# A WKV kernel on one core: k loads issued from GpSimd four pairs ahead, and the state chain in 12 VectorE operations a stage over four slots

## The chip, the core and the metric

The kernel runs on one core of a Trainium2 chip. The metric is the device time of one execution in microseconds (us); executions of one kernel differ by one to two per cent. An execution over 1.5% above the fastest of its kernel is counted as slow. All times compared here are of the state called fast, in which the core's mean granted TensorE clock is 0.96 to 0.99 of full speed. Where executions were slow, the text says so and gives the fast ones.

The engines are TensorE (PE; its weight loads are PEld), VectorE (DVE), ScalarE (ACT), GpSimd (POOL) and SyncE (SP). L258 is line 258 of the kernel that was profiled. The changed kernel has other line numbers.

## The reference, cut to what matters

```python
# k, v, out: (16, 2048, 256), float32; w, u: (256,)
for b in range(batch):
    aa, bb, pp = 0, 0, -1e38                  # per channel
    for t in range(seq_len):
        ww = u + k[b, t];  qq = max(pp, ww)
        e1, e2 = exp(pp - qq), exp(ww - qq)
        out[b, t] = (e1 * aa + e2 * v[b, t]) / (e1 * bb + e2 + 1e-08)
        ww = pp - w + k[b, t];  qq = max(ww, k[b, t])
        e1, e2 = exp(ww - qq), exp(k[b, t] - qq)
        aa, bb, pp = e1 * aa + e2 * v[b, t], e1 * bb + e2, qq
```

This is a weighted sum over all earlier steps, kept in range by a running maximum. The weight falls by `w` with each step.

## The kernel before

The kernel takes the 2048 steps in chunks of 126 (two halves of 63). One chunk of all 16 sequences is a **stage**. A stage has four **pairs** of four sequences each, and one pass of the main loop, a **slot**, brings one new pair in and takes an older one (ten slots back) out. The prediction calls the four slots of a stage A, B, C and D. In each slot:

- VectorE rounds k to float32r (`round_k`, "the k cast", L258), casts v to bf16 (L285), multiplies the exponentials by v (L293), and multiplies numerators by reciprocals, two halves per pair (L483).
- TensorE makes the logarithms of the weights (`X`, L266), sums per half chunk (`tot`, L323), numerators (`num`, L475) and denominators (`den`, L457).
- ScalarE makes `ez = exp(X)` (L277) and the reciprocal as exp(-ln) (L465, L466).

Between stages a state per sequence, channel and half chunk is carried on by small VectorE operations of 32 to 128 columns. The sums are turned by TensorE, so that channels lie along partitions (`turn_sums`, L339), and copied (`tsum`, L346). Logarithms give offsets `S`, exponentials of the offsets give weights, and the chain makes the state `AB`. The state is weighted again, turned back and put by four small DMAs into rows of `ez`, where the next outputs use it.

```python
def state_offsets(c):                         # five operations in slot A
    ...
    K(DVE.tensor_copy(S[:, 0, :], st.pop((c - 1, "S"))[:, 2, :]))
    for h in range(2):
        K(DVE.scalar_tensor_tensor(S[:, h + 1, :], S[:, h, :], 0.0, lf[:, h, :], ALU.max, ALU.add))
    K(DVE.tensor_scalar(ex[:, 0:2, :], S[:, 1:3, :], -1.0, 0.0, ALU.mult, ALU.max))
    K(DVE.scalar_tensor_tensor(ex[:, 2:4, :], S[:, 1:3, :], 0.0, lf, ALU.max, ALU.subtract))
...
def state_chain(c):                           # five operations in slot A
    ...
    K(DVE.tensor_mul(tb, t, g[:, 2:4, :]...))
    for h in range(2):
        dst = cur[:, :, 1, :] if h == 0 else nxt[:, :, 0, :]
        K(DVE.tensor_mul(da, cur[:, :, h, :], g[:, h:h + 1, :]...))
        K(DVE.tensor_add(dst, da, tb[:, :, h, :]))
...
def inject_min(c):                            # two operations at the end of slot A
    K(DVE.tensor_scalar(m, st.pop((c, "y")), -0.5, 0.5 * (CAP - LNRS), ALU.mult, ALU.add))
    K(DVE.scalar_tensor_tensor(m2, st[c, "S"][:, 0:2, :], 0.0, m, ALU.max, ALU.min))
...
def carries(c):                               # two multiplies in slot B
    for h in range(2):
        K(DVE.tensor_mul(ab[:, h]..., cur[:, :, h, :]..., f[:, h, :]...))
...
# when it runs: s = last slot of stage c
work += [(s + 1, "last", split_sums), (s + 2, "first" if c else "exp", state_logs),
         (s + 2, "sums", state_offsets), (s + 2, "sums", state_weights), (s + 2, "pool", state_chain),
         (s + 2, "act", inject_logs), (s + 3, "first", inject_min), (s + 3, "exp", inject_weights),
         (s + 3, "pool", carries), (s + 3, "last", turn_carries), (s + 3, "last", inject)]
```

The order within a slot is fixed by the main loop. Every operation is pinned behind the one before it on its engine.

```python
for n in range(NP + LAG + 1):
    load(n + AHEAD)                           # k and v, both issued by SP
    small_work(n, "first");  exps(n);  small_work(n, "exp")
    sums(n - 1);  round_k(n + 1);  small_work(n, "sums")
    num(qp, 0);  den(q);  recip(q);  mult(qp, 0);  num(qp, 1)
    small_work(n, "pool")
    times_v(n);  mult(qp, 1);  store(qp)      # stores: GpSimd; so are the row injections
    logs(n + 1);  cast_v(n + 1)
    small_work(n, "dve");  small_work(n, "act");  small_work(n, "last")
```

## Time and profile before

The median of three executions was 352.86 us (352.79 to 353.68). The profiled one took 353.72 us at a mean clock of 0.965.

| before, 352.0 us span | |
|---|---|
| busy: TensorE, VectorE, ScalarE, GpSimd | 82%, 84%, 79%, 28% |
| period of one stage (four k casts) | 18.67 us |
| spacing of the k casts in A, B, C, D | 6.27, 4.33, 3.53, 4.54 us |
| from the k cast at 85.73 us to the last, 48 casts (twelve stages) later | 223.36 us |
| DMA rate in one stage | 332 GB/s |

The whole-span shares say little, since three engines and the DMA engines all lie between 79 and 89%. The useful unit is the stage, and in it the question is which engine waits for which. The prediction reads those views. These lines are the timeline of VectorE in slot A and of TensorE in slot C (start, duration, engine, line, operation, output<-inputs with shapes and count; idle time just before and its releaser stand in brackets if there was any):

```profile
118.92 0.28 DVE L387 TENSOR_TENSOR tb<-tsum,g 128x128 f32<-128x128 f32 x1
...
119.89 0.22 DVE L392 TENSOR_TENSOR AB<-da,tb 128x64 f32<-128x64 f32 x1
120.03 1.22 DVE L293 TENSOR_TENSOR ez<-ez,vb 126x2048 bf16<-126x2048 bf16 x1
...
125.91 0.40 PE L323 MATMUL tot<-ez,OHE 128*48 128x512 bf16 x1
...
128.39 0.38 PE L475 MATMUL num<-ez,LfN 128*128 128x512 bf16 x1
```

The chain lasts from 118.92 to 120.03, where the v multiply (L293) begins, or 1.11 us.

### The profile page before, as it was taken

The numbers are of one execution on the slowest core, as the hardware profiler recorded it, in microseconds if no ns is written. First come the engines' busy times: TensorE is split into PE (matmuls) and PEld (weight loads), VectorE is DVE, ScalarE is ACT, GpSimd is POOL, SyncE is SP. The second block draws the span as 40 slices with busy tenths as digits, with TensorE's granted clock in tenths as the row PEclk, the third lists the DMA queues.
The fourth block names the chain that finished last, engine by engine and source line by source line (L and its number), as shares of the span: only waits on it lengthen the run. The fifth ranks groups of instructions, "written<-read, shape, count | busy, mean of one in ns | idle before, by whom it ended". The sixth has DMA issues, their size and how long they took to land.

```text
span 352.0 us, 4191 instructions
## 1 busy us (share of the span) xinstructions
PE 290.1 (82%) x1200; PEld 139.0 (39%) x1200; DVE 297.2 (84%) x636; ACT 278.8 (79%) x286; POOL 100.0 (28%) x164
## 2 busy tenths in 40 slices
PE   0578977788989898998989897979798989887870
PEld 0325433343434444444434353534354444433320
DVE  2666787889999999999999999999999999986551
ACT  2465557778988989898989888898888898987880
POOL 5000006131414140414233140514141405142630
PEclk9995689999999999999999999999999999999995
DMA  7899677699999989999999999999999999533774
GB/s 221 202 354 304 190 236 223 214 303 305 321 361 337 371 298 372 299 369 309 351 345 330 349 323 345 327 338 339 354 326 361 304 330 307 208 121 119 225 236 130
DMA packets 81366, 102.59 MB, mean 291 GB/s; under 512 B 5504, under 2 KB 73152, under 8 KB 81344
## 3 DMA queue, kind: packets, MB, share of 16 engines
q1 hardware_dynamic: 68160, 67.58, 60.3%
q0 software_dynamic: 12496, 34.11, 27.8%
q10 hardware_dynamic: 688, 0.66, 0.8%
q8 instruction: 9, 0.15, 0.2%
q14 instruction: 13, 0.11, 0.1%
HBM read 68.22 MB, written 33.55 MB: 289 GB/s over the span
## 4 chain that ended last, share of the span: by engine, by line
PE 40%; DVE 28%; issue 4%; ACT 3%; DMA 2%; POOLq 0%; DVEq 0%
PE num L475 11%; PE X L266 10%; DVE rd L483 8%; PE den L457 7%; PE tot L323 7%; DVE km L258 5%; DVE ez L293 5%; PE den L339 4%; DVE vb L285 2%; DVE AB L392 2%; DMA ez<-row 2%; ACT rd L466 2%; ACT rd L465 1%; DVE da L391 1%; DVE S L366 1%
## 5 line engine op out<-in xcount | busy, mean ns | idle before, releaser
L277 ACT ACTIVATE ez<-X 128x2048 bf16<-128x2048 f32 x66 | 122.2, 1852 | 22.8 <-PE X L266 22.8
L499 POOL DMA_DIRECT2D out_dram<-rd x64 | 58.6, 916 | 195.5 <-DVE rd L483 67.9
L483 DVE TENSOR_TENSOR rd<-num,rd 126x512 f32<-126x512 f32 (+1 forms) x131 | 88.6, 682 | 12.6 <-ACT rd L466 8.4
L293 DVE TENSOR_TENSOR ez<-ez,vb 126x2048 bf16<-126x2048 bf16 (+1 forms) x66 | 79.8, 1209 | 7.9 <-ACT ez L277 6.5
L465 ACT ACTIVATE rd<-den 126x1024 f32<-126x1024 f32 (+1 forms) x66 | 66.8, 1012 | 19.9 <-PE den L457 19.9
L466 ACT ACTIVATE rd<-rd 126x1024 f32<-126x1024 f32 (+1 forms) x66 | 69.5, 1052 | 2.1
L475 PE MATMUL num<-ez,LfN 128*128 128x512 bf16 x128 | 48.9, 382 | 21.4 <-DVE rd L483 20.8
L266 PE MATMUL X<-km,NLE 128*128 128x512 f32 x128 | 54.0, 505 | 15.1 <-DVE km L258 12.7
L323 PE MATMUL tot<-ez,OHV 126*48 126x512 bf16 x128 | 51.0, 399 | 8.5 <-DVE ez L293 8.5
L258 DVE CAST km<-kr 126x1024 fp32r<-126x1024 f32 x64 | 50.7, 792 | 4.6 <-ACT km L192 4.6
L323 PE MATMUL tot<-ez,OHE 128*48 128x512 bf16 x128 | 51.9, 405 | 0.0
L475 PE MATMUL num<-ez,IdN 126*128 126x512 bf16 (+1 forms) x131 | 49.8, 380 | 0.0
L285 DVE CAST vb<-vr 126x1024 bf16<-126x1024 f32 (+1 forms) x66 | 44.7, 677 | 3.3 <-DMA vr<-in_v_dram 3.3
L433 POOL DMA_DIRECT2D ez<-row x64 | 33.0, 520 | 46.7 <-DVE km L258 46.7
L266 PE MATMUL X<-km,NLZ 128*128 128x512 f32 x128 | 41.9, 410 | 0.0
L457 PE MATMUL den<-ez,Id 126*128 126x512 bf16 (+1 forms) x131 | 39.6, 382 | 0.0
L457 PE MATMUL den<-ez,Lf 128*128 128x512 bf16 x128 | 38.1, 378 | 1.5 <-DMA ez<-row 1.5
L266 PEld LDWEIGHTS X<-km,NLE 128*128 128x128 f32 x128 | 24.8, 201 | 28.7 <-DVE km L258 9.6
L475 PEld LDWEIGHTS <-IdN 126*128 126x128 bf16 (+1 forms) x131 | 12.7, 97 | 40.0 <-issue 38.6
L266 PEld LDWEIGHTS X<-km,NLZ 128*128 128x128 f32 x128 | 25.4, 199 | 6.1
L323 PEld LDWEIGHTS <-OHE 128*48 128x48 bf16 x128 | 13.4, 104 | 33.8 <-issue 27.0
L475 PEld LDWEIGHTS <-LfN 128*128 128x128 bf16 x128 | 12.3, 96 | 31.4 <-issue 22.7
(95 smaller groups left out, 199.5 us busy)
## 6 DMA issues: line engine op xcount, KB each, us to landing
out_dram<-rd POOLq DMA_DIRECT2D x64, 504.0 KB, 7.2
kr<-in_k_dram SPq DMA_DIRECT2D x60, 512.0 KB
vr<-in_v_dram SPq DMA_DIRECT2D x59, 512.0 KB
kr<-in_k_dram SPq DMA_DIRECT2D x4, 504.0 KB
vr<-in_v_dram SPq DMA_DIRECT2D x4, 504.0 KB
ez<-row POOLq DMA_DIRECT2D x64, 8.0 KB, 6.9
vr<-in_v_dram ACTq DMA_DIRECT2D x1, 512.0 KB
kr<-in_k_dram SPq DMA_DIRECT2D x3, 128.0 KB
```

The costliest lines, as they stand in the source:

```text
L258: K(DVE.tensor_copy(KM[n][0:r, 0:i, :], kr_of.pop(n)[0:r, 0:i, :]))
L266: K(PE.matmul(X[:, q, i, :], m[0:kr, :], km[0:kr, i, :], start=True, stop=True))
L277: K(SC.activation(ez_of(n)[:, 0:4:2], X_of.pop(n)[:, :, 0:i, :], ACT.Exp))
L285: K(DVE.tensor_copy(vb[0:r, 0:i, :], vr_of.pop(n)[0:r, 0:i, :]))
L293: K(DVE.tensor_mul(ez[0:r, 1:4:2], ez[0:r, 0:4:2], vb[0:r, 0:i, :].unsqueeze(1).broadcast_to([r, 2, i, D])))
L323: K(PE.matmul(TOT[c], m[0:r, :], ez_of(n)[0:r, q, i, :], start=n == first_of[c] and i == 0 and q == 0, stop=n == last_of[c] and i == tiles ...
L457: K(PE.matmul(d[:, i, :], m[0:r, :], ez_of(n)[0:r, q, i, :], start=q == 0, stop=q == 2, skip_group_check=True))
L465: K(SC.activation(rd[0:r, 0:i, :], DEN.pop(n)[0:r, 0:i, :], ACT.Ln, scale=RS))
L466: K(SC.activation(rd[0:r, 0:i, :], rd[0:r, 0:i, :], ACT.Exp, scale=-1.0))
L475: K(PE.matmul(d, m[0:r, :], ez_of(n)[0:r, q, i, :], start=q == 1, stop=q == 3, skip_group_check=True))
L483: K(DVE.tensor_mul(RD[n][0:r, i, :], NUM.pop((n, i))[0:r, :], RD[n][0:r, i, :]))
L499: K(POOL.dma_start(out=out[4 * p:4 * p + 4, t0:t0 + TC, :].rearrange("n t d -> t n d"), in_=o[0:TC, :, :]))
```

## The change

The change has two parts. First, k loads go out on GpSimd's queue, four pairs ahead with four buffers, where they went on SP's queue three ahead with four. The row injections go to SP in exchange. Second, the state chain is rewritten. Offsets stay in one tile for all stages (no copy), and the exponentials become exponentials of one clamped offset. Minima and maxima are folded into the multiplies that use them, and the `m` pair goes. The second step of the chain is moved to slot C. The intent is fewer VectorE operations per stage, set where they hurt less. The core of the diff, with the head of the sequence and unchanged lines left out:

```diff
-    AHEAD = 3
+    AHEAD = 4
-    kpool = ...(name="kpool", bufs=AHEAD + 1)       # vpool likewise
+    kpool = ...(name="kpool", bufs=AHEAD)
-            for t, x, eng in ((kr, k, SP), (vr, v, SP if n else SC)):
+            for t, x, eng in ((kr, k, SP if n <= AHEAD else POOL), (vr, v, SP if n else SC)):
 ...
+    S = consts.tile([128, 2 * NST + 1, 32], F32, tag="S", name="S")
     def state_offsets(c):
-        (copy S, two S, two ex: see above)
+        for h in range(2):
+            i = 2 * c + h
+            K(DVE.scalar_tensor_tensor(S[:, i + 1], S[:, i], 0.0, lf[:, h], ALU.max, ALU.add))
+        K(DVE.tensor_scalar(near, S[:, 2 * c:2 * c + 3], NEAR, -NEAR, ALU.min, ALU.max))
     def state_weights(c):
-        K(SC.activation(g[:, sl, :], st.pop((c, "ex"))[:, sl, :], ACT.Exp, scale=-2.0))
+            K(SC.activation(w, near[:, 0:2], ACT.Exp, scale=-2.0))
+            K(SC.activation(g, near, ACT.Exp, scale=2.0))
-    def state_chain(c):
-        (tb, then da and AB twice: see above)
+    def state_step(c, h):
+        if h == 0:
+            K(DVE.scalar_tensor_tensor(tb, by_two(st.pop((c, "w"))), 1.0, t, ALU.min, ALU.mult))
+        ...
+        K(DVE.tensor_add(da, cur[:, :, h], st[c, "tb"][:, :, h]))
+        K(DVE.scalar_tensor_tensor(cur[:, :, 1] if h == 0 else AB[c + 1][:, :, 0],
+                                   by_two(st[c, "g"][:, h + 1]), 1.0, da, ALU.min, ALU.mult))
-    def inject_min(c):
-        (m, m2: see above)
     def inject_weights(c):
-        K(SC.activation(f, st.pop((c, "m")), ACT.Exp, scale=2.0))
+        K(SC.activation(f, st.pop((c, "y")), ACT.Exp, scale=-1.0, bias=cc[:, 5:6]))
     def carries(c):
-        for h in range(2):
-            K(DVE.tensor_mul(ab[:, h]..., cur[:, :, h, :]..., f[:, h, :]...))
+        K(DVE.scalar_tensor_tensor(f2, st[c, "g"][:, 0:2], 1.0, f, ALU.max, ALU.min))
+        K(DVE.tensor_mul(ab, AB[c]..., f2...))
     def inject(c):
-                K(POOL.dma_start(out=EZ[group_of(c, j)]...
+                K(SP.dma_start(out=EZ[group_of(c, j)]...
 ...
-                     (s + 2, "sums", state_offsets), (s + 2, "sums", state_weights), (s + 2, "pool", state_chain),
-                     (s + 2, "act", inject_logs), (s + 3, "first", inject_min), (s + 3, "exp", inject_weights),
+                     (s + 2, "sums", state_offsets), (s + 2, "sums", state_weights), (s + 2, "pool", first),
+                     (s + 2, "act", inject_logs), (s + 3, "exp", inject_weights),
+            if c + 1 < NST:
+                work.append((s + 4 if c else s + 3, "pool", second))
```

More of the change, by code (lines that the diff above doesn't have):

```diff
@@ L64 @@
     CAP = 68.0
+    NEAR = 44.0
     consts = ctx.enter_context(tc.tile_pool(name="consts", bufs=1))
-    kpool = ctx.enter_context(tc.tile_pool(name="kpool", bufs=AHEAD + 1))
-    vpool = ctx.enter_context(tc.tile_pool(name="vpool", bufs=AHEAD + 1))
+    kpool = ctx.enter_context(tc.tile_pool(name="kpool", bufs=AHEAD))
+    vpool = ctx.enter_context(tc.tile_pool(name="vpool", bufs=AHEAD))
     vbpool = ctx.enter_context(tc.tile_pool(name="vbpool", bufs=2))
@@ L161 @@
     K(POOL.memset(cc[:, 4:5], 0.5))
+    K(POOL.memset(cc[:, 5:6], CAP - LNRS))
     select(cc[:, 4:5], GE, 0.0, -HS, 1, 1, 0)
@@ L187 @@
     K(DVE.scalar_tensor_tensor(NLE[:, TC + 1:128], cc[:, 2:3], -0.5 * HS, cc[:, 4:5], ALU.mult, ALU.add))
-    for n in range(2, AHEAD + 1):
+    for n in range(2, AHEAD):
         load(n)
@@ L347, in split_sums @@
         st[c, "t"] = t
+    S = consts.tile([128, 2 * NST + 1, 32], F32, tag="S", name="S")
     def state_logs(c):
+        if c < 0:
+            K(SC.activation(S[:, 0], st[c, "t"][:, 4], ACT.Ln))
+            return
         lf = tiny.tile([128, 2, 32], F32, tag="lf", name="lf")
-        H = 1 if c < 0 else 2
-        K(SC.activation(lf[:, 0:H], st[c, "t"][:, 4:4 + H], ACT.Ln))
+        K(SC.activation(lf, st[c, "t"][:, 4:6], ACT.Ln))
         st[c, "lf"] = lf
@@ L357, in state_offsets, with state_weights @@
         lf = st.pop((c, "lf"))
-        S = small.tile([128, 3, 32], F32, tag="S", name="S")
-        ex = tiny.tile([128, 4, 32], F32, tag="ex", name="ex")
+        for h in range(2):
+            i = 2 * c + h
+            K(DVE.scalar_tensor_tensor(S[:, i + 1], S[:, i], 0.0, lf[:, h], ALU.max, ALU.add))
+        near = tiny.tile([128, 3, 32], F32, tag="near", name="near")
+        K(DVE.tensor_scalar(near, S[:, 2 * c:2 * c + 3], NEAR, -NEAR, ALU.min, ALU.max))
+        st[c, "near"] = near
+    def state_weights(c):
+        g = small.tile([128, 3, 32], F32, tag="g", name="g")
@@ L360, in state_offsets @@
         if c < 0:
-            K(DVE.tensor_copy(S[:, 2, :], lf[:, 0, :]))
-            K(DVE.scalar_tensor_tensor(ex[:, 2, :], S[:, 2, :], 0.0, lf[:, 0, :], ALU.max, ALU.subtract))
-        else:
-            K(DVE.tensor_copy(S[:, 0, :], st.pop((c - 1, "S"))[:, 2, :]))
-            for h in range(2):
-                K(DVE.scalar_tensor_tensor(S[:, h + 1, :], S[:, h, :], 0.0, lf[:, h, :], ALU.max, ALU.add))
-            K(DVE.tensor_scalar(ex[:, 0:2, :], S[:, 1:3, :], -1.0, 0.0, ALU.mult, ALU.max))
-            K(DVE.scalar_tensor_tensor(ex[:, 2:4, :], S[:, 1:3, :], 0.0, lf, ALU.max, ALU.subtract))
@@ L369, in state_offsets @@
-        st[c, "S"] = S
-        st[c, "ex"] = ex
-    def state_weights(c):
-        g = tiny.tile([128, 4, 32], F32, tag="g", name="g")
-        sl = slice(2, 3) if c < 0 else slice(0, 4)
-        K(SC.activation(g[:, sl, :], st.pop((c, "ex"))[:, sl, :], ACT.Exp, scale=-2.0))
-        st[c, "g"] = g
-    def state_chain(c):
-        g, t = st.pop((c, "g")), st.pop((c, "t"))[:, 0:4].rearrange("p (q h) x -> p q h x", q=2)
-        nxt = small.tile([128, 2, 2, 32], F32, tag="AB", name="AB")
-        if c < 0:
-            K(DVE.tensor_mul(nxt[:, :, 0, :], t[:, :, 0, :], g[:, 2:3, :].broadcast_to([128, 2, 32])))
-        else:
-            cur = AB[c]
-            tb = tiny.tile([128, 2, 2, 32], F32, tag="tb", name="tb")
-            K(DVE.tensor_mul(tb, t, g[:, 2:4, :].unsqueeze(1).broadcast_to([128, 2, 2, 32])))
-            for h in range(2):
-                dst = cur[:, :, 1, :] if h == 0 else nxt[:, :, 0, :]
-                da = tiny.tile([128, 2, 32], F32, tag=f"da{h}", name=f"da{h}")
-                K(DVE.tensor_mul(da, cur[:, :, h, :], g[:, h:h + 1, :].broadcast_to([128, 2, 32])))
-                K(DVE.tensor_add(dst, da, tb[:, :, h, :]))
-        AB[c + 1] = nxt
+            K(SC.activation(g[:, 0], S[:, 0], ACT.Exp, scale=2.0))
+        else:
+            w = tiny.tile([128, 2, 32], F32, tag="w", name="w")
+            near = st.pop((c, "near"))
+            K(SC.activation(w, near[:, 0:2], ACT.Exp, scale=-2.0))
+            K(SC.activation(g, near, ACT.Exp, scale=2.0))
+            st[c, "w"] = w
@@ new lines, in state_weights, with by_two, state_start @@
+        st[c, "g"] = g
+    def by_two(x):
+        n = list(x.shape)
+        return x.unsqueeze(1).broadcast_to([n[0], 2] + n[1:])
+    def state_start(c):
+        AB[0] = small.tile([128, 2, 2, 32], F32, tag="AB", name="AB")
+        t = st.pop((c, "t"))[:, 0:4].rearrange("p (q h) x -> p q h x", q=2)
+        K(DVE.scalar_tensor_tensor(AB[0][:, :, 0], by_two(st.pop((c, "g"))[:, 0]), 1.0, t[:, :, 0],
+                                   ALU.min, ALU.mult))
+    def state_step(c, h):
+        if h == 0:
+            t = st.pop((c, "t"))[:, 0:4].rearrange("p (q h) x -> p q h x", q=2)
+            tb = small.tile([128, 2, 2, 32], F32, tag="tb", name="tb")
+            K(DVE.scalar_tensor_tensor(tb, by_two(st.pop((c, "w"))), 1.0, t, ALU.min, ALU.mult))
+            st[c, "tb"] = tb
+        cur = AB[c]
+        if h == 1:
+            AB[c + 1] = small.tile([128, 2, 2, 32], F32, tag="AB", name="AB")
+        da = tiny.tile([128, 2, 32], F32, tag=f"da{h}", name=f"da{h}")
+        K(DVE.tensor_add(da, cur[:, :, h], st[c, "tb"][:, :, h]))
+        K(DVE.scalar_tensor_tensor(cur[:, :, 1] if h == 0 else AB[c + 1][:, :, 0], by_two(st[c, "g"][:, h + 1]), 1.0,
+                                   da, ALU.min, ALU.mult))
@@ L398, in inject_logs @@
         st[c, "y"] = y
-    def inject_min(c):
-        m = tiny.tile([128, 2, 32], F32, tag="m", name="m")
-        K(DVE.tensor_scalar(m, st.pop((c, "y")), -0.5, 0.5 * (CAP - LNRS), ALU.mult, ALU.add))
-        m2 = tiny.tile([128, 2, 32], F32, tag="m2", name="m2")
-        K(DVE.scalar_tensor_tensor(m2, st[c, "S"][:, 0:2, :], 0.0, m, ALU.max, ALU.min))
-        st[c, "m"] = m2
     def inject_weights(c):
         f = tiny.tile([128, 2, 32], F32, tag="phi", name="phi")
-        K(SC.activation(f, st.pop((c, "m")), ACT.Exp, scale=2.0))
+        K(SC.activation(f, st.pop((c, "y")), ACT.Exp, scale=-1.0, bias=cc[:, 5:6]))
         st[c, "phi"] = f
     def carries(c):
-        ab = tiny.tile([128, 2, 2, 2, 16], BF16, tag="ab16", name="ab16")
-        cur, f = AB.pop(c), st.pop((c, "phi"))
-        for h in range(2):
-            K(DVE.tensor_mul(ab[:, h].rearrange("p j q x -> p q j x"),
-                             cur[:, :, h, :].rearrange("p q (j x) -> p q j x", j=2),
-                             f[:, h, :].rearrange("p (j x) -> p j x", j=2).unsqueeze(1).broadcast_to([128, 2, 2, 16])))
+        ab = tiny.tile([128, 4, 2, 16], BF16, tag="ab16", name="ab16")
+        f, f2 = st.pop((c, "phi")), tiny.tile([128, 2, 32], F32, tag="phi2", name="phi2")
+        K(DVE.scalar_tensor_tensor(f2, st[c, "g"][:, 0:2], 1.0, f, ALU.max, ALU.min))
+        K(DVE.tensor_mul(ab, AB[c].rearrange("p q h (j x) -> p (h j) q x", j=2),
+                         f2.rearrange("p h (j x) -> p (h j) x", j=2).unsqueeze(2).broadcast_to([128, 4, 2, 16])))
         st[c, "ab"] = ab
@@ L423, in turn_carries @@
         d = bank("den", [128, 2, D])[:, 0]
-        K(PE.matmul(d[:, 0:128], st.pop((c, "ab")).rearrange("p h j q x -> p (h j q x)"), Id, start=True, stop=True))
+        K(PE.matmul(d[:, 0:128], st.pop((c, "ab")).rearrange("p m q x -> p (m q x)"), Id, start=True, stop=True))
         st[c, "d"] = d
@@ L432, in inject @@
                 p = 64 * h + 32 * j
-                K(POOL.dma_start(out=EZ[group_of(c, j)][TC + h:TC + h + 1, 0:2, :, :].rearrange(
+                K(SP.dma_start(out=EZ[group_of(c, j)][TC + h:TC + h + 1, 0:2, :, :].rearrange(
                                    "o q i (x c) -> o (q i x) c", c=128),
@@ L506 @@
         work = [(s + 1, "sums", copy_sums), (s + 1, "last", turn_sums)]
+        first, second = lambda c: state_step(c, 0), lambda c: state_step(c, 1)
         if c < 0:
-            work += [(s + 2, "sums", split_sums), (s + 2, "act", state_logs), (s + 2, "last", state_offsets),
-                     (s + 3, "exp", state_weights), (s + 3, "pool", state_chain)]
+            work += [(s + 2, "sums", split_sums), (s + 2, "act", state_logs),
+                     (s + 3, "exp", state_weights), (s + 3, "pool", state_start)]
         else:
             work += [(s + 1, "last", split_sums), (s + 2, "first" if c else "exp", state_logs),
-                     (s + 2, "sums", state_offsets), (s + 2, "sums", state_weights), (s + 2, "pool", state_chain),
-                     (s + 2, "act", inject_logs), (s + 3, "first", inject_min), (s + 3, "exp", inject_weights),
+                     (s + 2, "sums", state_offsets), (s + 2, "sums", state_weights), (s + 2, "pool", first),
+                     (s + 2, "act", inject_logs), (s + 3, "exp", inject_weights),
                      (s + 3, "pool", carries), (s + 3, "last", turn_carries), (s + 3, "last", inject)]
+            if c + 1 < NST:
+                work.append((s + 4 if c else s + 3, "pool", second))
         for slot, where, f in work:
@@ L537 @@
             widen()
-        if 0 < n and n + AHEAD < NP:
+        if n + AHEAD < NP:
             load(n + AHEAD)
```

## The prediction

> **What bounds the kernel now.** I read the page first: busy shares, then the slices.
>
> ```profile
> PE 290.1 (82%) x1200; PEld 139.0 (39%) x1200; DVE 297.2 (84%) x636; ACT 278.8 (79%) x286; POOL 100.0 (28%) x164
> DVE  2666787889999999999999999999999999986551
> DMA  7899677699999989999999999999999999533774
> ```
>
> The average hides the shape: VectorE is at 90% or more from slice 11 to slice 35, and so are the DMA engines. TensorE and ScalarE are only some points behind. So there is a long steady part, and four resources in it lie close together. The starts of the k casts (one per pair of sequences) repeat in that part with a period of four pairs, one "stage": 6.27, 4.33, 3.53 and 4.54 us apart, 18.67 us in all. I call these slots A, B, C, D. The busy times in one stage:
>
> ```profile
> core 0: us, PE busy (x) PEld busy (x) DVE busy (x) ACT busy (x) POOL busy (x), PEclk, DMA share, GB/s
> ...
> 117.33:136.00 18.67, 16.88 (x75) 8.20 (x74) 17.89 (x37) 16.62 (x18) 5.72 (x8) 1.00 0.96 332
> ```
>
> To see who sets the period I asked for the chain of waits of this stage alone:
>
> ```profile
> 116.55 0.89 DVE km L258
> ...
> 118.40 0.60 DVE rd L483
> ...
> 122.73 0.44 DVE km L258
> 123.18 0.48 issue
> 123.66 0.68 DVE rd L483
> ...
> 124.39 0.59 PE num L475 x2
> ...
> 133.79 1.04 PE den L339 x8
> ...
> 134.85 0.36 DVE tsum L346
> 135.21 0.89 DVE km L258
> ```
>
> The stage is two runs in series. From the k cast of A to the first output multiply of B (116.46 to 124.34, 7.88 us) VectorE works without a gap and TensorE waits for it. From the numerator matmul at 124.39 to the turning of the sums, which begins at 133.73 and ends near 134.8, TensorE runs back to back through B, C and D, 10.4 us; in C and D VectorE waits for it. What is removed from VectorE counts only in the first run. What is added in C counts as soon as VectorE has no slack there.
>
> One thing more is visible in the order of time of VectorE and GpSimd:
>
> ```profile
> 122.37 0.18 DVE L402 TENSOR_SCALAR m<-y 128x64 f32<-128x64 f32 x1
> 122.44 0.81 POOL L499 DMA_DIRECT2D out_dram<-rd  x1 [5.50 <-DVE rd L483]
> 122.73 1.01 DVE L258 CAST km<-kr 126x1024 fp32r<-126x1024 f32 x1
> ...
> 130.59 0.68 DVE L258 CAST km<-kr 126x1024 fp32r<-126x1024 f32 x1
> 130.70 0.91 POOL L499 DMA_DIRECT2D out_dram<-rd  x1 [0.60 <-DVE vb L285]
> ```
>
> A k cast takes 0.68 us, but 1.01 (slot B) or 0.97 (slot A) when small operations stand between the v cast and it: GpSimd then gets to its store issue first, and the cast ends only when the issue ends. Where the k cast follows at once, or after one small operation (slots C, D and 126.9), VectorE loses nothing and the issue takes 0.91 or 1.15 us.
>
> **What the Trainium skill says.** "SBUF — State Buffer", section "Who interferes with whom", says that VectorE copies, casts and tensor_scalars in a two-port mode and GpSimd take one shared port pair by an exclusive lock, and that whoever issues first holds it for its whole instruction; it adds that issuing the DMA from another queue avoids this. The trace agrees (1.01 against 0.68 us). "VectorE: DVE Perf Modes", "Rules for kernel authors", advises to reduce the count of operations, since the drain between them is paid anyway; the trace agrees: a 64-column operation costs 0.22 to 0.26 us from start to start if it needs the one before, 0.11 to 0.14 if not. "DMA: Bandwidth & Descriptors", section "Issuing engines are not separate DMA queues", says that all issuers share the same 16 DMA engines. So moving k loads to GpSimd makes no bandwidth. No line of this trace tests that, but the DMA share of 0.96 in the stage above says that it matters.
>
> **The change part by part.** Start-to-start times from the stage at 116.46 to 135.13.
>
> 1. Slot A, offsets: one copy, two S, two ex (117.36 to 118.32, 0.96 us) become two S and one clamp of 96 columns: 0.25 + 0.25 + 0.14 = 0.64. Saves 0.32.
> 2. Slot A, chain: tb, da, AB, da, AB (118.92 to 120.03, 1.11 us) become tb, da, AB. Now da needs tb: 0.32 + 0.26 + 0.14 = 0.72. ScalarE makes two exponentials (64 and 96 columns) where one of 128 took 0.30, and tb may wait some 0.15 for the first. Saves 0.24.
> 3. Slot A, the two m operations before the k cast of B (122.37 to 122.73): gone, 0.36 saved. With them goes what let GpSimd in first: the cast of B should take 0.68 again, 0.33 saved.
> 4. Slot B: two ab multiplies (124.26 to 124.52, 0.26 us) become f2 and ab in series, 0.26 + 0.20. This lies beside TensorE's run: 0.20 more busy time, nothing on the path.
> 5. Slot C takes the second da and AB, 0.26 + 0.14 = 0.40. C is the slot where VectorE is already full (3.53 us for operations that sum to 3.54). TensorE's numerator in C waits for a multiply behind the k cast, and the next slot's sums wait for the v multiply behind the new pair. Following the order of both engines through C and D by hand, TensorE's run becomes 0.28 longer.
> 6. k loads on GpSimd: four issues per stage added, which I take as long as a store's (0.83 us median; same bytes within 2%), four row injections of 0.51 us removed. GpSimd goes from 5.7 to about 7 us per stage. The order of its instructions puts each k load behind the store of the slot before, so two issues follow each other, 1.7 us. In B, C and D the second one lies beside multiplies, which the trace shows undisturbed by issues. In A the sums' copy still stands before the k cast, so that cast stays at 0.97, and the clamp of part 1 can meet the k load's issue: I add 0.15.
>
> Sum on the path: -0.32 - 0.24 - 0.36 - 0.33 + 0.28 + 0.15 = -0.82 us per stage, 17.85 in place of 18.67. Twelve stages run in this regime (from about 85 to 309 us): -9.8. Three stages before that have the same operations but idle gaps besides: I allow -0.3 each, -0.9. The start of the outputs waits once for the injected rows (TensorE, 1.5 us near 58 us); SP is free to issue them earlier: -0.3. The last 42 us are a drain in which TensorE, two ScalarE steps and a multiply follow each other at 4.38 us per pair; nothing of the change is in it. 352.9 - 11.0 = 341.9, rounded to 342.
>
> The prefetch itself should show nothing: in the steady part VectorE never waits for a load now. A k load goes out when its cast frees the buffer (117.47) and is used at 135.13, 17.7 us later; behind the store it goes out some 3 us later, leaving about 14. A store takes 7.1 us to land on GpSimd's queue. "Four ahead" with four buffers is the same memory as three ahead with four.
>
> **The rivals.**
> - *The DMA engines become the bound.* A stage moves 4 x (512 + 512 + 504) KB, 6.26 MB: 335 GB/s at 18.67 us, 351 at 17.85. For it: the share is already near 1. Against: whole slices of the page ran at 369 to 373 GB/s, and in the stage above the rate falls below 200 for stretches of half a microsecond around 124 and 129, so there is slack. If 335 were the ceiling, nothing would be gained: 352. If it is 345, a stage takes 18.1 us: 345.
> - *More lock collisions.* Eight large issues per stage in place of four large and four small. If each k load cost the next cast 0.33 as a store does now, a stage would lose 1.3 us: slower, 358. Against it is the order: the k load's issue falls on multiplies. One collision per stage more than I count would make 346.
> - *TensorE takes all of the period.* Its own work is 16.9 us per stage and its run in C and D has no slack. If the first run shrinks further than I think (no stall in A either), the period still can't go under about 17: 332. I hold this unlikely, as C becomes a VectorE slot.
>
> **Range and chances.** The first three parts rest on measured spacings; the two additions are by hand and could be 0 or 0.7 us per stage together, which is 8 us over twelve stages. 337 to 349 covers that and a mild DMA bound. 2% is 345.8. Chances: 0.77 faster, 0.20 within, 0.03 slower, the last for collisions of the second rival.
>
> **What would show it.** Right: a period near 17.8 us of the k casts, slot A near 5.4 and slot C near 3.9; the k cast of B at 0.68 and that of A still near 0.97; 12 small VectorE operations per stage in place of 16; no wait of a cast for a load. Wrong: casts waiting for k (DMA bound or GpSimd late); casts or the clamp at 1 us in several slots, with GpSimd issues over them; slot C or D longer than the time saved in A; or an unchanged period with the chain wholly on TensorE.

## More of the kernel before

In slot C, TensorE needs 2.48 us from the first sum to the numerator of C. That numerator stands without a bracket: TensorE was never idle before it.

## The result

The changed kernel took 340.31 us in the median of four executions (338.74 to 343.80), against 353.27 (352.79 to 355.17) for the kernel before beside it. Ratios here are the mean time of one kernel's fast runs over that of the other's of the same rounds, so they are not quite the ratio of the medians quoted. This one is 0.9637, with a 95% interval from 0.9553 to 0.9721. The profiled execution was the slowest of the four: 343.8 us, span 342.1, clock 0.965.

| | before | after |
|---|---|---|
| period of one stage | 18.67 us | 17.77 us |
| k cast spacing A, B, C, D | 6.27, 4.33, 3.53, 4.54 | 5.45, 4.20, 3.93, 4.19 |
| small VectorE operations per stage | 16 | 12 |
| k cast of A, of B | 0.97, 1.01 us | 0.77, 0.69 us |
| GpSimd busy per stage | 5.72 us | 6.88 us |
| k cast to k cast over the same twelve stages | 223.36 us | 213.34 us |
| before that stretch; after it | 85.73; 42.9 us | 85.03; 43.7 us |

The gain lies in the steady part, where the twelve stages became 10.0 us shorter. The stretches before and after it hardly moved in these two profiles. The early stretch is also where executions of one kernel differ: in a second profile of the changed kernel (338.26 us, told below) the same k cast started at 81.1 us where it was 85.0, while the steady parts of both agree within 0.1 us (213.34 and 213.3). Periods are therefore a better measure of the change than single times.

The page of the changed kernel, busy shares and two rows of the 40 slices (busy tenths):

```profile
PE 292.4 (85%) x1200; PEld 139.7 (41%) x1200; DVE 283.2 (83%) x568; ACT 279.4 (82%) x302; POOL 114.0 (33%) x162
...
DVE  2465796898989898989999999999998989886451
...
DMA  7799775989999999999999999999999999844675
```

VectorE is no longer the busiest engine: 568 instructions where there were 636, 14 us less busy. TensorE has the same 1200 instructions and now the largest share.

The busy times in one stage (the columns are those of the same view in the prediction):

```profile
168.41:186.18 17.77, 16.86 (x75) 8.20 (x73) 16.81 (x34) 16.61 (x18) 6.88 (x9) 1.00 1.02 355
```

VectorE lost 1.08 us per stage, TensorE and ScalarE nothing. All three stand at 93 to 95% of the period. The DMA rate rose from 332 to 355 GB/s in the same four columns at the end.

The chain of waits of this stage (start, duration, engine, what):

```profile
168.53 0.26 ACT lf L360
168.78 1.02 ACT ez L279
...
170.45 0.26 ACT w L379
...
170.72 0.30 DVE tb L399
...
175.20 0.59 PE num L482 x2
...
177.94 0.20 DVE row L436
178.14 0.60 DVE km L260
178.74 0.61 DVE rd L490
...
184.85 1.03 PE den L341 x8
...
185.91 0.37 DVE tsum L348
```

In before this chain went through VectorE alone from the k cast of A to the multiply of B. Now it begins in ScalarE: logarithm, the big exponential of slot A, then `w`, and only then VectorE's `tb`. The second half, from `num` to the turning of the sums (`den L341`), ran on TensorE alone in before. Now it passes through VectorE in slot C (`row`, the k cast and a multiply, 1.4 us), before TensorE takes over again: VectorE has no slack there.

The timeline of VectorE and GpSimd in the same stage, for the lines shown of before:

```profile
167.85 0.83 POOL L506 DMA_DIRECT2D out_dram<-rd  x1 [1.85 <-ACT rd L473]
168.41 0.77 DVE L260 CAST km<-kr 126x1024 fp32r<-126x1024 f32 x1
168.68 0.80 POOL L122 DMA_DIRECT2D kr<-in_k_dram  x1
...
173.86 0.69 DVE L260 CAST km<-kr 126x1024 fp32r<-126x1024 f32 x1
173.96 0.92 POOL L506 DMA_DIRECT2D out_dram<-rd  x1 [4.48 <-ACT y L411]
```

The k cast of B (173.86) now starts before the store's issue and takes 0.69 us. The k cast of A (168.41) starts 0.56 us into the issue of the store and loses only 0.09. The k load's issue at 168.68 follows the store's, and costs VectorE nothing here. The k loads land in 8.1 us in the median, and no k cast of the steady part waits for one.

### The profile page after: what moved, and what is told of

It is laid out like the page before. It is cut to its first block, busy times and chain, and to the rows that moved or that the text cites. A ratio compares the mean times of both kernels' runs of the same rounds, so it can differ in the third digit from the quotient of the medians.

```text
span 342.1 us, 4063 instructions
## 1 busy us (share of the span) xinstructions
PE 292.4 (85%) x1200; PEld 139.7 (41%) x1200; DVE 283.2 (83%) x568; ACT 279.4 (82%) x302; POOL 114.0 (33%) x162
## 4 chain that ended last, share of the span: by engine, by line
PE 48%; DVE 26%; ACT 14%; issue 5%; DMA 3%; ACTq 0%; POOLq 0%; DVEq 0%
PE X L268 15%; PE tot L325 11%; PE num L482 11%; ACT ez L279 8%; DVE rd L490 6%; DVE ez L295 6%; PE den L464 6%; DVE km L260 5%; PE den L341 5%; DMA vr<-in_v_dram 3%; DVE vb L287 3%; ACT rd L472 2%; ACT rd L473 2%; DVE tsum L348 2%; DVE tb L399 1%
## 5 line engine op out<-in xcount | busy, mean ns | idle before, releaser
L122 POOL DMA_DIRECT2D kr<-in_k_dram x61 | 47.8, 784 | 39.4 <-DVE km L260 20.4
L260 DVE CAST km<-kr 126x1024 fp32r<-126x1024 f32 x64 | 44.7, 699 | 4.8 <-ACT km L194 4.8
```

The costliest lines, as they stand in the source:

```text
L260: K(DVE.tensor_copy(KM[n][0:r, 0:i, :], kr_of.pop(n)[0:r, 0:i, :]))
```

## The experiments

Kernels ran beside the same kernel before: 352.52 us in the median, 352.64, 353.14. "Period" is the spacing of k casts over one stage in the profile. In most stages it repeats within 0.02 us; a few stages differ by some tenths (one of the changed kernel takes 17.91), and the last one, which passes into the drain, can be longer still.

### The queues alone

The kernel before, with only the k loads on GpSimd, four ahead, and the row injections on SP:

```diff
-    AHEAD = 3
+    AHEAD = 4
-    kpool = ...(name="kpool", bufs=AHEAD + 1)       # vpool likewise
+    kpool = ...(name="kpool", bufs=AHEAD)
-            for t, x, eng in ((kr, k, SP), (vr, v, SP if n else SC)):
+            for t, x, eng in ((kr, k, SP if n <= AHEAD else POOL), (vr, v, SP if n else SC)):
-                K(POOL.dma_start(out=EZ[group_of(c, j)]...
+                K(SP.dma_start(out=EZ[group_of(c, j)]...
```

> The kernel before with only the queue half of the change: k loads on GpSimd from pair 5 on, four pairs ahead with the same four buffers, row injections on SP. Theory (GpSimd and VectorE lock each other out, and bandwidth is not the limit): the k casts of slots A and B stay at 0.97 and 1.0 us, since the small operations still stand before them, and the second issue behind each store may also meet the small two-port operations; period 18.5 to 19.0 us, time 350 to 357. Rival (the two queues feed the DMA engines better and that is where the gain comes from): period near 17.8, time below 345.

Measured: 350.09 us, ratio 0.9949 (0.9884 to 1.0013). The period is 18.54 us in most stages (A 6.46, B 4.01, C 3.54, D 4.53), with some from 18.30 to 18.89; the twelve stages take 222.55 us, where they took 223.36. Time and period are in the expected band. The queues are worth about 0.1 us per stage here and nothing that the interval can tell from zero. One expectation missed: the k cast of B took 0.69 us, not 1.0, though the order of operations around it is that of before. The timeline shows why:

```profile
176.37 0.19 DVE L402 TENSOR_SCALAR m<-y 128x64 f32<-128x64 f32 x1
176.47 1.29 POOL L499 DMA_DIRECT2D out_dram<-rd  x1 [4.93 <-issue]
...
176.73 0.69 DVE L258 CAST km<-kr 126x1024 fp32r<-126x1024 f32 x1
```

The cast started 0.26 us after the store's issue; in before it was 0.29 (122.44 and 122.73 in the prediction's lines) and the cast took 1.01. Here the cast is not held and the issue is stretched to 1.29. So whether this cast is held is decided within a few hundredths of a microsecond. In A the k load's issue now delayed the copy of `S`: it took 0.36 us instead of 0.16.

### The chain alone

The changed kernel, with the queues and the depth of before:

```diff
-    AHEAD = 4
+    AHEAD = 3
-            for t, x, eng in ((kr, k, SP if n <= AHEAD else POOL), (vr, v, SP if n else SC)):
+            for t, x, eng in ((kr, k, SP), (vr, v, SP if n else SC)):
-                K(SP.dma_start(out=EZ[group_of(c, j)]...
+                K(POOL.dma_start(out=EZ[group_of(c, j)]...
```

> The changed kernel with the old queues: all loads on SP, three ahead, injections on GpSimd; only the state chain is new. Theory: nearly the whole gain is here, period 17.7 to 17.9, time 339 to 344. Rival (queues give the gain): above 348. If the queues give a small part (an earlier store issue, injections that land sooner): 342 to 346.

Measured: 342.20 us, ratio 0.9699 (0.9635 to 0.9762). The period is 17.77 us, slot by slot that of the changed kernel (5.45, 4.20, 3.92, 4.18). Time and period are as expected. The steady gain is wholly the chain's.

### Both again, side by side

To see whether the queues add anything to the chain, the changed kernel and the chain alone ran again:

> The changed kernel itself, again, so that the next runs are compared with it on one chip. Period 17.77, time 339 to 342.

> The chain half alone, beside the changed kernel on the same chip. Theory: with the new chain the queues are worth nothing in the steady part (both periods were 17.77), so the two times agree within 0.5% (1.7 us). Rival (the queue half still gives 2 us, as the first comparison across two chips suggests, 0.9699 against 0.9637): 1.5 to 3 us slower than the changed kernel.

Measured: the changed kernel 339.4 us in its four fast executions (340.64 with two that count as slow, at clocks of 0.97 like the others), ratio 0.9618 (0.9544 to 0.9691); the chain alone 341.56, ratio 0.9665 (0.9607 to 0.9723). Both have a period of 17.77 us. The ratios differ by 0.0047, or 1.7 us, which falls between the theory and the rival, and the intervals overlap. The first comparison had the same sign (0.9637 and 0.9699). So a gain of some 2 us from the queues is neither shown nor ruled out. What there may be of it lies outside the steady part.

### The m operations later

The prediction put 0.33 us of slot B down to the port lock. If the small `m` operations in front of the k cast let GpSimd in first, then putting them behind the cast in the kernel before should free the cast:

```diff
-        (s + 3, "first", inject_min), (s + 3, "exp", inject_weights),
+        (s + 3, "sums", inject_min), (s + 3, "sums", inject_weights),
```

> The kernel before, with the two m operations moved from in front of the k cast of slot B to behind it; no operation added or removed. Theory (small operations before the cast let GpSimd's issue take the shared ports first): the k cast of B falls from 1.0 to 0.68 us, that of A stays at 0.97, the period falls by 0.33 to about 18.35, time about 349 (347.5 to 350.5). Rival (the 1.0 us is something else, or the time is taken back in the next slot): 352 to 354.

Measured: 352.51 us in five fast executions (a sixth was slow), ratio 1.0002 (0.9945 to 1.0060); period 18.57 (A 5.90, B 4.60, C 3.53, D 4.54). The time is a miss: it lies in the rival's band, that the time is taken back. The timeline of VectorE and GpSimd around the cast of B:

```profile
160.62 0.69 DVE L258 CAST km<-kr 126x1024 fp32r<-126x1024 f32 x1
160.69 0.95 POOL L499 DMA_DIRECT2D out_dram<-rd  x1 [5.50 <-DVE rd L483]
161.22 0.41 DVE L402 TENSOR_SCALAR m<-y 128x64 f32<-128x64 f32 x1
```

The cast is free, as expected. But the stall did not vanish: `m`, the next operation of the kind that meets the lock, took 0.41 us instead of 0.18 under the same issue. ScalarE then waited 0.96 us for `m`, so the weights of the carries came later. Slot A won 0.37 and slot B lost 0.27. So removing the pair, as the change does, is worth more than moving it.

### The second step back in slot A

The changed kernel, with the second `da` and `AB` directly behind the first:

```diff
-                work.append((s + 4 if c else s + 3, "pool", second))
+                work.insert(7, (s + 2, "pool", second))
```

> The changed kernel with the second step of the chain back behind the first in slot A. Theory of the two runs in series (VectorE through A to the multiply of B, then TensorE through B, C, D): slot A grows by 0.5, slot C falls from 3.93 to about 3.55, the TensorE run shortens by 0.24; period 17.77 + 0.50 - 0.24 = 18.0, time about +3 us on the changed kernel: 343 to 345. Rival (VectorE's sum alone sets the period, the place does not matter): period 17.8, same time as the changed kernel within 1 us.

Measured: 347.26 us in three fast executions (a fourth was slow), ratio 0.9841 (0.9779 to 0.9903); period 18.24 (A 5.97, B 4.20, C 3.54, D 4.53). A is 0.52 longer and C is 0.39 shorter, as expected. D is 0.34 longer, which was not foreseen, and so the period missed its 18.0 and the time its 343 to 345. C and D together take 8.07 us here and 8.12 with the second step in C. The step costs 0.05 us in C, not the 0.28 of the prediction: TensorE sets the length of C plus D, and what VectorE adds in C it no longer waits for in D. The spreading alone is worth 0.47 us per stage, half of the whole gain.

### Without the clamp of the carries

If f2 and ab lie on the path, taking f2 away must shorten a stage by about its 0.24 us. The result is wrong (relative error 0.79):

```diff
-        f, f2 = st.pop((c, "phi")), tiny.tile([128, 2, 32], F32, tag="phi2", name="phi2")
-        K(DVE.scalar_tensor_tensor(f2, st[c, "g"][:, 0:2], 1.0, f, ALU.max, ALU.min))
+        f2 = st.pop((c, "phi"))
```

> The changed kernel without the clamp f2 in front of the carries of slot B (one VectorE operation less per stage; the result is wrong where the clamp binds). The prediction's fourth part said that these operations lie beside TensorE's run and cost nothing. Theory now, from the trace (VectorE runs without a gap from slot B's multiply to slot C's, and TensorE's numerator of C waits for that multiply): 0.20 to 0.25 less per stage, period about 17.55, time about 3 us below the changed kernel's 340.6. Rival (the prediction's part 4): period 17.77, no change.

Measured: the three fast runs took 335.73 to 338.61 us, ratio 0.9552 (0.9497 to 0.9608). The fourth, the profiled one, was slow (473.73 us, granted clock 0.571), so its period tells nothing. Against the changed kernel's 0.9618, on another chip, that is 0.0066 less, or 2.3 us, near the 3 us that twelve stages of 0.24 make. The intervals overlap, and the next run shows as much (0.9555) with an unchanged period. So this run settles nothing.

### Without the wait for w

The chain of waits puts `tb` behind ScalarE's `w`. Here `tb` takes a constant instead (wrong, relative error 0.89), and `w` is still computed:

```diff
+    ONE = consts.tile([128, 2, 32], F32, tag="ONE", name="ONE")
+    K(POOL.memset(ONE, 2.0 ** -20))
-            K(DVE.scalar_tensor_tensor(tb, by_two(st.pop((c, "w"))), 1.0, t, ALU.min, ALU.mult))
+            K(DVE.scalar_tensor_tensor(tb, by_two(ONE), 1.0, t, ALU.min, ALU.mult))
```

> The changed kernel with a constant in place of the first weights w in tb, so that tb waits for no ScalarE operation (wrong result; w is still computed). Theory (the wait of 0.46 us for w in slot A is on the path): the v multiply of A starts 0.46 earlier, and TensorE then takes over after some 0.33; period 17.3 to 17.45, 4 to 5.5 us below the changed kernel. Rival (slot A is set by ScalarE's big exponential or by TensorE anyway): period above 17.7.

Measured: 337.68 us, ratio 0.9555 (0.9504 to 0.9605), and a period of 17.77 us, unchanged (A 4.98, B 4.67, C 3.92, D 4.20). The expectation for the period is missed; the rival's, above 17.7, is met. A became 0.47 shorter and B 0.47 longer. The timeline of VectorE in B says what took the place of the wait:

```profile
170.12 0.23 DVE L426 SCALAR_TENSOR_TENSOR phi<-g,phi 128x64 f32<-128x64 f32 x1 [0.37 <-ACT phi L419]
```

The clamp f2 (`phi<-g,phi`) now waits 0.37 us for ScalarE. ScalarE's own run from the logarithm `lf` to the end of `phi` takes 6.49 us here (163.60 to 170.09) and took the same 6.49 in the changed kernel (168.53 to 175.02), where f2 started at 175.07, as VectorE came free. So two runs tie in A and B of the changed kernel, VectorE's and ScalarE's, and shortening one of them brings nothing. By the ratios the time was 2.2 us better than that of the changed kernel. The period doesn't show that, it may be the early stretch, and it stays open.

### The chain one slot later

A rearrangement to get rid of the wait: `lf` goes behind slot A's exponential, and everything after it one slot later.

```diff
-            work += [(s + 1, "last", split_sums), (s + 2, "first" if c else "exp", state_logs),
-                     (s + 2, "sums", state_offsets), (s + 2, "sums", state_weights), (s + 2, "pool", first), ...
+            e = 1 if c else 0
+            work += [(s + 1, "last", split_sums), (s + 2, "exp", state_logs),
+                     (s + 2 + e, "sums", state_offsets), (s + 2 + e, "sums", state_weights), (s + 2 + e, "pool", first), ...
-                work.append((s + 4 if c else s + 3, "pool", second))
+                work.append((s + 5 if c else s + 3, "pool", second))
```

> The changed kernel with the logarithm of the sums behind the exponentials of slot A on ScalarE, and the whole chain one slot later. Theory: in slot A of the changed kernel ScalarE's big exponential waits 0.68 us behind the small logarithm for the turned sums, and VectorE then waits for ScalarE; without that the exponential starts at once, period 17.2 to 17.5, time 334 to 338. Rival (TensorE's own run is the whole bound, VectorE and ScalarE only lean on it): period 17.7 to 17.8, no gain. Second rival (the wait for the first weights comes back in slot B, where the same three operations now stand): period about 17.5.

Measured: 339.25 us in three fast executions (a fourth was slow), ratio 0.9633 (0.9568 to 0.9697); period 17.68 (5.06, 4.20, 4.19, 4.24). The expected 17.2 to 17.5 is missed, and the first rival's 17.7 to 17.8 nearly met. The wait for `w` is down to 0.16 us, but now a multiply of slot A waits 0.60 us for its numerator (the trace puts it down to `lf`, which had ended at 164.16; the numerator ended at 164.29 and the multiply began at 164.38) and ScalarE waits 1.03 us for denominators: TensorE, 16.87 us busy of 17.70, leads instead. Only 0.09 us per stage was won.

### Turning the sums in one pass, in the changed kernel and in before

TensorE's end of the path is the turning of the sums, four float32 matmuls. They can be had as float32r:

```diff
+    I1r = matrix("I1r", F32R)
+        K(DVE.tensor_copy(I1r, I1))
-        ts = small.tile([48, D], F32, tag="ts", name="ts")
+        ts = small.tile([48, D], F32R, tag="ts", name="ts")
-            K(PE.matmul(..., ts[:, 128 * d:128 * d + 128], I1[0:48, 0:48],
+            K(PE.matmul(..., ts[:, 128 * d:128 * d + 128], I1r[0:48, 0:48],
```

> The changed kernel with the four float32 matmuls that turn the sums (8 passes, 1.03 us per stage, at the end of TensorE's run) in float32r, one pass each. May be less exact. Theory (the turning lies on the path at the end of TensorE's run, before VectorE's sums copy and k cast of slot A): 0.4 to 0.6 us less per stage, period 17.2 to 17.4, time 333 to 337. Rival (slot A is set by ScalarE or by VectorE, so the sums come earlier and wait): period above 17.6.

Measured: correct, 333.87 us (331.52 to 334.67), ratio 0.9456 (0.9400 to 0.9511). The period is 17.37 us: D falls from 4.19 to 3.80, and A, B and C stay. The timeline of TensorE shows the turning of one stage in the changed kernel, then in this one:

```profile
184.78 1.09 PE L341 MATMUL den<-I,ts 48*128 48x48 f32 x8
```

```profile
161.03 0.62 PE L344 MATMUL den<-I1r,ts 48*128 48x48 f32 x4
```

Eight matmul records became four and 1.09 us became 0.62. Nearly all of the 0.47 shows in the period (0.40), so TensorE's run is what sets the end of D. Period and time are as expected. The kernel is 5.6 us under the fast executions of the changed kernel, 4.8 of it in twelve stages, and the intervals do not touch: this version beats both kernels.

The same edit in the kernel before:

> The kernel before with the sums turned in float32r and nothing else. Theory (the prediction's reading of before: the turning ends TensorE's run, and VectorE starts slot A after it): 0.3 to 0.45 less per stage, period 18.2 to 18.4, time about 348. Rival (before is VectorE bound throughout, as its busy row of 90% suggests): within 1 us of before.

Measured: 347.82 us, ratio 0.9875 (0.9800 to 0.9950); period 18.42 (A 6.22, B 4.32, C 3.53, D 4.34), 0.25 shorter where 0.3 to 0.45 had been expected, and a time as expected. The turning was on the path of before too. A kernel whose VectorE is the busiest engine got 1.3% faster by an edit to TensorE: the two runs in series are real. That only 0.25 came of it has two reasons in this run's trace. With the shorter turning, the chain of waits runs through VectorE in the second half of D (its v multiply, multiply and v cast). And the k cast of A, now free of the lock (0.68 us), hands its stall to the next copy, which takes 0.40 us where it took 0.16:

```profile
169.04 0.40 DVE L367 COPY S<-S 128x32 f32<-128x32 f32 x1
```

### One-pass turning and the later chain together

The last two edits in one kernel:

> Both candidates together: the sums turned in float32r, and the chain one slot later with the logarithm behind slot A's exponentials. Theory: the turning gave 0.40 per stage and the shift 0.09 alone; together the waits of slot A and of the den matmuls shrink too: period 17.1 to 17.3, time 329 to 333. Rival (VectorE, busy about 16.9 us per stage, is full by then, or the DMA engines at 6.26 MB per stage are): 17.3 to 17.4, no better than the turning alone at 333.9.

Measured: correct, 333.10 us (330.71 to 335.50), ratio 0.9432 (0.9369 to 0.9494), which the interval can't tell from one-pass turning alone. The period is 17.22 us in most stages, as expected, but four take 17.4 to 18.1, and the last, which passes into the drain, 21.5. The chain of waits of the last has this piece:

```profile
263.04 11.44 DMA ez<-row
```

Rows of the state that were injected a slot later took 11.4 us to land (the median of all rows is 6.3), and the denominators had to wait for them: 3.5 us here, 4.8 over the whole run. The later chain alone shows such a wait once (3.2 us), the changed kernel and the one-pass turning none. So the later chain gives back part of what it wins to a transfer that had been hidden.

## Why the prediction was right, and where its sum was not

The time (342.0 against 340.3), the period (17.85 against 17.77) and the direction were right. The main reading held: two runs in series, of which the first, VectorE's, shrinks. But four terms of the sum were off by 0.18 us or more (parts 2, 4, 5 and 6), and their errors cancelled: that the sum came out is luck. Of the signs that were named, only that of the k cast of A (still near 0.97; it took 0.77) failed. The stages compared are those at 116.46 to 135.13 (before) and 168.41 to 186.18 (after), read off starts in the timelines; the rest between the two runs is 0.37 us in both, and sums agree within the rounding of 0.01.

| part of the prediction | predicted | measured |
|---|---|---|
| 1. offsets in A (117.36 to 118.32; 169.10 to 169.66) | -0.32 | 0.96 to 0.56: -0.40 |
| 2. chain in A (118.92 to 120.03; 170.26 to 171.53) | -0.24 | 1.11 to 1.27: +0.16 |
| 3. m pair gone, cast of B free | -0.36 - 0.33 | -0.36 - 0.32 |
| 6. clamp under the k load's issue; cast of A | +0.15; cast unchanged | 0; cast's slot 0.90 to 0.69: -0.21 |
| first run, sum | -1.10 | 7.87 to 6.74: -1.13 |
| 4. f2 and ab in B | 0 on the path | +0.18 |
| 5. second step in C | +0.28 | +0.05 |
| second run, sum | +0.28 | 10.43 to 10.67: +0.24 |
| stage | -0.82 | -0.90 |

**Part 1** was right. Two `S` and a clamp took 0.56 us; the estimate from the old spacings was 0.64.

**Part 2 failed**: "saves 0.24". In its place, the chain of three operations takes longer than that of five. The timeline of VectorE in A:

```profile
170.72 0.29 DVE L399 SCALAR_TENSOR_TENSOR tb<-w,tsum 128x128 f32<-128x128 f32 x1 [0.38 <-ACT w L379]
171.05 0.23 DVE L405 TENSOR_TENSOR da<-AB,tb 128x64 f32<-128x64 f32 x1
171.39 0.22 DVE L406 SCALAR_TENSOR_TENSOR AB<-g,da 128x64 f32<-128x64 f32 x1
```

The multiply before it was started at 169.66 and at its usual 0.60 us the chain could begin at 170.26. It began 0.46 later, of which the trace marks 0.38 as idle: `w` is behind the big exponential in ScalarE's order, and that is behind `lf` (chain of waits above). The wait had been set at 0.15. From start to start `tb`, `da` and `AB` then take 0.33, 0.34 and 0.14 (0.32, 0.26 and 0.14 predicted). The shorter offsets of part 1 are in this wait too: VectorE came to `tb` earlier, and ScalarE did not. So is the shorter cast of part 6: in the run with one-pass turning the k cast of A was shorter again (0.68 us), the wait grew to 0.46, and A stayed at 5.45. The run without the wait shows moreover that this term is not free to be won: without it ScalarE's run to `phi` holds the period at 17.77.

**Part 3** was right in both terms. One reading in it is not what its lines show: the delayed cast does not end when the issue ends (122.44 + 0.81 = 123.25) but 0.49 us later (122.73 + 1.01 = 123.74). That the k cast of B is free of the lock comes from the order (the cast starts 0.10 us before the issue). The run with `m` moved shows that such a stall passes on to the next operation that can meet it. The change removes both `m` operations, so that no such operation follows the cast of B.

**Part 4 failed**: "this lies beside TensorE's run: 0.20 more busy time, nothing on the path". It is on the path. The timeline of TensorE in C, for the two lines of before:

```profile
176.73 0.40 PE L325 MATMUL tot<-ez,OHE 128*48 128x512 bf16 x1
...
179.39 0.38 PE L482 MATMUL num<-ez,LfN 128*128 128x512 bf16 x1 [0.17 <-DVE rd L490]
```

It took 2.66 us where it was 2.48, and the numerator now waits 0.17 us for a VectorE multiply. From the multiply of B to that of C VectorE runs without a gap in both kernels, 4.00 us in before (123.66 to 127.66) and 4.19 after (174.47 to 178.66), longer by what f2 and ab add. In before the multiply of C ended at 128.34 and the numerator started at 128.39, when TensorE had just finished the denominators (128.38). A numerator that does wait starts just as long after its multiply (124.34 and 124.39 in the prediction's chain), so both engines were ready at the same moment: VectorE had no slack, and was not "beside". TensorE without idle time was read as VectorE with slack. The reading of the timelines carries the point, not the run without f2.

**Part 5** had the right sign and a size five times too large: the term is 0.05, not 0.28. From the numerator of C to the end of the turning TensorE takes 6.48 us, where it took 6.43. C became 0.40 longer by VectorE's two operations, and D shorter by 0.35, because VectorE had been waiting there. The run with the step back in slot A measures the same 0.05 from the other side. That parts 4 and 5 together came out at +0.23 against +0.28 is luck, and so is that the 0.36 by which part 6 was better made up for the 0.40 by which part 2 was worse.

**Part 6**: the issues on GpSimd are as predicted (0.78 us for a k load, 6.88 us busy per stage). The collision of the clamp did not come: the k load's issue ended at 169.48 and the clamp began at 169.53, 0.05 us later. The cast of A got 0.20 us shorter, which was not foreseen: the store's issue starts 0.7 us after the v cast in both kernels, but in the changed one VectorE then waits 0.30 us for TensorE's turning, so the k cast comes later against the issue (0.56 us after its start instead of 0.35) and meets less of it. What the cast no longer loses to the lock stands in front of it as a wait for TensorE.

**The ends.** -0.9 for the early stages and -0.3 for the start of the outputs can't be checked: two executions of the changed kernel differ by 4 us there. The medians of the two kernels are 13.0 us apart and their steady parts 10.0. The other 3 us must lie in the ends, and nothing here explains them beyond that spread. The drain is 42.9 and 43.7 us in the first two profiles and 42.2 in the second of the changed kernel: unchanged, as predicted.

**The rivals.** The DMA engines are no bound at these rates: 355 GB/s in the stage, 378 in the best slice, no k cast waiting. (The prediction's 369 to 373 for slices of before is 369 to 372 on that page.) Lock collisions did not increase in the changed kernel. In before with the new queues alone, one (the copy of `S`) did appear, and one fell away. TensorE taking all of the period was held unlikely, and is the nearest to the truth of what comes next: 16.86 us of 17.77 are its own, and both edits behind it (one pass for the turning, the chain a slot later) point to it. But it does not hold the whole period: its shorter turning moved D alone, and A to C, where the chain of waits passes through ScalarE and VectorE as well, stayed.

## What to carry to other kernels

An engine that runs without a gap does not prove that the engine feeding it has slack: compare the end of what it needs with its start, at the place where the new work goes. When a chain loses operations, look at what its first operand waits for on the other engine, since the operations removed may only make the wait longer. And once three engines stand at 95% of a period, look for the end of the one run that all return to: here two tile types in TensorE's turning gave 5.6 us, 0.40 per stage, where taking away VectorE's wait for `w` gave nothing per stage and the later chain 0.09.

## What the Trainium skill lacked or had wrong

- "SBUF — State Buffer", section "Who interferes with whom", says that the engine which issues first has the shared pair for its whole instruction. By the records of these runs the hold is shorter than the issue: k casts that started 0.15 us (in before with one-pass turning) and 0.26 us (in before with the new queues) after the store's issue began were not delayed (0.68 and 0.69 us) and the issue was stretched to 1.17 and 1.29; casts that started 0.29 and 0.35 us after it (before, B and A) took 1.01 and 0.97. The same border stands in thirteen traces, after the first 85 us: no k cast that started up to 0.28 us after an issue was held, and every one that started 0.29 to 0.62 us after it was. Every held cast ended 0.49 us after the recorded end of the issue, less than its own 0.68, so the pair comes free about 0.2 us before that end. The start and the end are read from the traces, the cause is an inference.
- The same section does not say that freeing one operation hands the stall to the next that can meet the lock: 0.41 us for a 64-column tensor_scalar instead of 0.18 when the cast in front of it was freed, and 0.40 for a 32-column copy instead of 0.16 in before with one-pass turning.
- "VectorE: DVE Perf Modes", section "Rules for kernel authors", advises to minimize the count of operations. Three chain operations in place of five took 1.27 us instead of 1.11 (a wait for ScalarE of 0.46 in it), and f2 with ab, two operations that depend on each other, took 0.45 where two independent ones took 0.26. The count alone decided neither.
- "FP8 and Floating Point Precision", section "TensorE Precision Notes", says that true float32 takes four passes, and that reduced-precision float32 is cut to about 22 bits. The trace shows two matmul records per float32 turning matmul, not four, and one per float32r matmul: 1.09 and 0.62 us for the four matmuls of a stage. Whether one record is one pass, no run here shows, nor the number of bits; the result stayed correct with the turned sums in float32r.
